# The depthwise convolution of the gated branch, issued step by step at a counted pace instead of with one late priority

## The chip, the core and the metric

The kernel runs on one NeuronCore of a Trainium2 chip. Five engines matter here: TensorE (matmuls, "PE" in the profile, its weight loads "PEld"), VectorE ("DVE"), ScalarE ("ACT"), GpSimd ("POOL") and SyncE ("SP", which only issues DMAs). Each works through its own instruction list in order and waits on semaphores for the others. The metric is the device time of one execution in microseconds. The kernel before the change takes 1662.74 us (median of 3 runs, 1662.30 to 1662.97).

## The reference, cut to what matters

```python
xn = rmsnorm(x, norm1_g)
proj = xn @ w_in
q, k, v, glu_a, glu_b, gate_a, gate_b = jnp.split(proj, SPLIT_IDX, axis=-1)
# branch A: sliding-window attention -> @ w_o_attn
u = glu_a * jax.nn.sigmoid(glu_b)                    # branch B, 1024 channels
u_ext = jnp.concatenate([conv_b_past, u], axis=1)    # 30 earlier rows
c = dwconv_valid(u_ext, conv_b_w, conv_b_bias)       # causal depthwise convolution, 31 taps
branch_b = jax.nn.silu(layernorm(c, ln_b_g, ln_b_b)) @ w_pb
merged = jax.nn.sigmoid(gate_a) * branch_a + jax.nn.sigmoid(gate_b) * branch_b
h = x + merged @ w_out
# then a feed-forward block with a 3-tap convolution, and a final RMSNorm
```

There are 1024 prompt tokens and 8 samples of 8 tokens, so 1088 columns, all in float32. A matmul is done as three: operands are split into a high part and a remainder, and high x high, high x remainder and remainder x high are added in PSUM (`mm3`, L201 to L203).

## The kernel before

**Stages.** The first stage (up to 649 us of the profile) is the input projection: 44 weight units of 128x1024 are streamed one after the other. The first five units, whose streams are interleaved, are not touched by the change. Every later unit but the two of the values makes one *stream*: three column chunks of 384, 384 and 320, eight contraction steps each, so 24 steps of three matmuls. The order of the units is the table `SEQUENCE`; `b` and `a` are the two halves of a gated unit (eight pairs, 0 to 7), `g` a gate, `q0`, `q1`, `k0`, `k1`, `v` the attention operands of two groups of heads. The later stages (attention output, branch-B projection, output projection, feed-forward) are not touched.

**What VectorE does in the first stage.** It takes the remainder of each weight unit (L183, `wlo`, after ScalarE has made the high part `whi`, L182), empties PSUM for q, k, v and the gated half (L731, L753, L231 `v`, L686), does most of the softmax (L330, L337), the remainders of the attention operands (L231 `ptl`, L388 `av`), and the convolution. One convolution (function `conv`, one of eight) has two products and two sums for the sample rows (L489, L490), one sum of neighbours (L491), 44 multiply-adds over 512 or 513 elements (L483; tiles `bt` and `c`) and four closing instructions (L502 to L505), 53 vector instructions in all. It ends with two stores to DRAM (`d_c`). Its three starting products are made on ScalarE.

**Buffers.** Two weight pairs (`whi`/`wlo` 0 and 1) alternate: the split of the next unit can begin once the unit before the present one has been streamed, and has to be done when its own stream starts. Two `u` tiles alternate between the eight gated units, so a convolution must be finished and stored before the unit two places on writes its `u`. PSUM has four `mm` banks, one for each chunk, and four `aux` banks for the attention.

**What sets the order.** The program is recorded in Python; each instruction gets a priority from its place in the record, and a scheduler at build time then arranges every engine's list, preferring what was recorded early among what it believes to be ready. `later(n)` lowers the priority of a block by n places. Small attention steps are planned on an agenda and recorded by `tick()`, which `stream` calls at each contraction step; `do_v`, which streams the two value units in nine blocks, doesn't call it. The whole of a convolution is recorded when its gated unit is complete (`a_done`, L689 to L694), under `later(CONV_LATER)` with 1200 places, so the scheduler fills it in wherever VectorE has nothing of better priority.

Of the kernel before, what the change touches and what calls it, by code (L numbers as in the profile page):

```python
# [74 lines left out]
CONV_LATER = 1200  # L75
# [45 lines left out]
class Build:  # L121
    def __init__(self, tc, a):
        self.tc, self.nc, self.a = tc, tc.nc, a
        self.order, self.n_in = weight_order()
        self.uid = 0
        self.agenda, self.now = [], 0

# [333 lines left out]
    def tick(self, upto=None):  # L461
        self.now = self.now + 1 if upto is None else upto
        while self.agenda and self.agenda[0][0] <= self.now:
            self.agenda.pop(0)[1]()

# [5 lines left out]
    def conv(self, i, u):  # L471
        nc = self.nc
# [13 lines left out]
        for x in range(2):  # L486
            win = us[:, 4 * x:4 * x + 4, 0:NT]
            win = bass.AP(tensor=win.tensor, offset=win.offset, ap=[list(z) for z in win.ap] + [[1, CW]])
            nc.vector.tensor_tensor(prod, win, taps, ALU.mult)  # L489
            nc.vector.tensor_reduce(sp[:, 4 * x:4 * x + 4, :], prod, AX.X, ALU.add)  # L490
        nc.vector.tensor_tensor(sm, od[:, 0:half + 15], ev[:, 1:half + 16], ALU.add)  # L491
# [4 lines left out]
        for j in range(1, 16):  # L496
            mac(bt, ev[:, j:j + half + 1], h(2 * j))
            if j < 15:
                mac(ye, od[:, j:j + half], h(2 * j + 1))
            mac(yo, sm[:, j:j + half], hs(j))  # L500
        out = u[:, NS:NS + SEQ]
        nc.vector.tensor_scalar(u[:, 0:NS], acc[:, SEQ:], self.c("cb", i), None, ALU.add)  # L502
        nc.vector.tensor_tensor(yo, yo, bt[:, 1:], ALU.subtract)
        nc.vector.tensor_tensor(out[:, 1::2], yo, ye, ALU.subtract)
        nc.vector.tensor_tensor(out[:, 0::2], ye, bt[:, 0:half], ALU.add)  # L505
# [136 lines left out]
    def phase_x(self):  # L642
# [17 lines left out]
        def u_start(i):  # L660
            u = self.t(self.cv, [P, UW], "u", bufs=2)
            nc.gpsimd.memset(u[:, 0:HIST], 0.0)
            nc.gpsimd.memset(u[:, HIST + SEQ:PW], 0.0)
            nc.sync.dma_start(u_views(u)[:, :, 0:HIST], a["cbT"][i])
            return u
# [23 lines left out]
        def a_done(i, u):  # L689
# [3 lines left out]
            with self.later(CONV_LATER):  # L693
                self.conv(i, u)  # L694
# [125 lines left out]
        u = u_start(0)  # L820
# [18 lines left out]
        for c in range(3):  # L839
# [9 lines left out]
            keep = [lambda c, o, n, ps, ev=ev: held.append(lambda: ev(c, o, n, ps)) for ev in evs]  # L849
# [68 lines left out]
    def phase_y(self, right, a0_es, states, ah, al):  # L918
# [22 lines left out]

        steps = []
# [864 lines left out]
```

## Time and profile before

| what | us |
|---|---|
| median of the runs | 1662.74 |
| the profiled execution, its own time | 1661.67 |
| its span, first to last instruction | 1659.9 |
| ACT busy in the span | 892.3 (54%) |
| POOL busy in the span | 318.4 (19%) |
| DVE busy in the span | 1338.7 (81%) |

The page gives busy time by engine, then the span in 40 slices with a digit for the busy tenths of each, then the chain of work that ended last, then groups of equal instructions. The trace can be asked for waits (who waited for whom, in total), for windows (busy time of each engine in a stretch) and for the timeline (instructions in order with the idle time ahead of them). The timeline's lines have start and duration in us, engine, source line, operation, output and inputs. [...]

### The profile page before, as it was taken

How to read it: one execution, taken by the hardware profiler on the slowest of the kernel's cores; microseconds unless marked ns; L12 is line 12 of the kernel's file. 1: busy time of each engine (PE TensorE's matmuls, PEld its weight loads, DVE VectorE, ACT ScalarE, POOL GpSimd, SP SyncE). 2: the span in 40 equal slices, each digit the busy share in tenths (PEclk: the TensorE clock that was granted, in tenths of full speed). 3: DMA queues.
4: the chain of work that ended last, by engine and by line, in shares of the span. 5: the costliest groups of instructions: out<-in, count | busy, mean ns of one | idle time of the engine just before them, and what ended most of it. 6: DMA issues, size and time to landing. Idle time of an engine off the chain costs nothing.

```text
span 1659.9 us, 30349 instructions
## 1 busy us (share of the span) xinstructions
PE 1641.4 (99%) x11616; PEld 1623.9 (98%) x11616; DVE 1338.7 (81%) x2432; ACT 892.3 (54%) x1819; POOL 318.4 (19%) x589
## 2 busy tenths in 40 slices
PE   9999999999999999999999999999999999999998
PEld 9999899999999999999999999999999999999998
DVE  8999988999769995875676897877777778968546
ACT  7524377753388754993353564444444446834322
POOL 0400222151211211110000123333433221000050
PEclk9999999999999999999999999999999999999999
DMA  6122135163421255545346527676777544856473
GB/s 213 46 48 71 60 94 136 48 200 82 124 67 49 66 192 189 176 137 187 120 126 204 134 71 212 182 182 176 182 176 176 144 112 142 288 158 220 137 147 119
DMA packets 121746, 232.12 MB, mean 140 GB/s; under 512 B 25457, under 2 KB 68097, under 8 KB 121169
## 3 DMA queue, kind: packets, MB, share of 16 engines
q1 hardware_dynamic: 88496, 140.01, 27.4%
q0 software_dynamic: 32384, 89.51, 21.3%
q8 instruction: 91, 1.49, 0.4%
q10 hardware_dynamic: 720, 0.66, 0.1%
q14 instruction: 55, 0.44, 0.1%
HBM read 169.74 MB, written 89.62 MB: 156 GB/s over the span
## 4 chain that ended last, share of the span: by engine, by line
PE 83%; DVE 11%; ACT 3%; DMA 1%; issue 1%; SPq 0%; DVEq 0%; ACTq 0%
PE mm L201 20%; PE mm L202 20%; PE mm L203 20%; PE aux L201 6%; PE aux L203 6%; PE aux L202 6%; DVE c L483 3%; DVE bt L483 1%; PE aux L369 1%; DMA xr<-xT 1%; DVE q L731 1%; PE aux L359 1%; DVE wlo L183 1%; PE aux L381 1%; DVE xr L307 1%
## 5 line engine op out<-in xcount | busy, mean ns | idle before, releaser
L201 PE MATMUL mm<-xh,whi 128*128 128x384 f32 (+1 forms) x920 | 306.7, 333 | 2.9 <-ACT kd L754 1.6
L203 PE MATMUL mm<-xh,wlo 128*128 128x384 f32 (+1 forms) x920 | 300.6, 327 | 0.0
L202 PE MATMUL mm<-xl,whi 128*128 128x384 f32 (+1 forms) x920 | 300.5, 327 | 0.0
L201 PEld LDWEIGHTS mm<-xh,whi 128*128 128x128 f32 x920 | 173.0, 188 | 5.1 <-ACT kd L754 1.9
L202 PEld LDWEIGHTS mm<-xl,whi 128*128 128x128 f32 x920 | 173.2, 188 | 0.8
L203 PEld LDWEIGHTS mm<-xh,wlo 128*128 128x128 f32 x920 | 172.7, 188 | 0.1
L1225 DVE SCALAR_TENSOR_TENSOR acc<-st,fc,acc 128x1104 f32<-128x1104 f32 x88 | 119.5, 1362 | 8.7 <-ACT acc L1223 7.9
L182 ACT CAST whi<-wraw 128x1024 fp32r<-128x1024 f32 (+1 forms) x65 | 62.6, 969 | 55.8 <-PE mm L202 49.6
L483 DVE SCALAR_TENSOR_TENSOR bt<-u,consts,bt 128x513 f32<-128x513 f32 x120 | 89.7, 748 | 0.6
L483 DVE SCALAR_TENSOR_TENSOR c<-sm,hsum,c 128x512 f32<-128x512 f32 x120 | 89.5, 746 | 0.5
L183 DVE TENSOR_TENSOR wlo<-wraw,whi 128x1024 fp32r<-128x1024 f32 (+1 forms) x65 | 73.3, 1134 | 20.1 <-ACT whi L182 19.7
L483 DVE SCALAR_TENSOR_TENSOR c<-u,consts,c 128x512 f32<-128x512 f32 x112 | 83.5, 746 | 0.3
L230 ACT CAST wlo<-th 128x512 fp32r<-128x512 f32 x56 | 35.1, 626 | 65.1 <-PE aux L203 41.4
L1394 ACT COPY st<-mm 128x272 f32<-128x272 f32 (+2 forms) x133 | 44.4, 350 | 46.7 <-PE mm L203 46.7
L201 PE MATMUL mm<-th,whi 128*128 128x272 f32 x240 | 69.3, 289 | 0.0
L203 PE MATMUL mm<-th,whi 128*128 128x272 f32 x240 | 69.3, 289 | 0.0
L202 PE MATMUL mm<-tl,whi 128*128 128x272 f32 x240 | 69.1, 288 | 0.0
L335 ACT ACTIVATE p<-p,nm 128x257 f32<-128x257 f32 (+1 forms) x128 | 62.2, 490 | 12.0 <-DVE nm L330 11.2
L1373 DVE TENSOR_TENSOR st<-st,aux 128x272 f32<-128x272 f32 (+2 forms) x95 | 34.2, 379 | 38.0 <-PE aux L203 38.0
L203 PE MATMUL mm<-sh,wlo 128*128 128x384 f32 (+1 forms) x192 | 62.6, 326 | 0.0
L202 PE MATMUL mm<-sl,whi 128*128 128x384 f32 (+1 forms) x192 | 62.6, 326 | 0.0
L201 PE MATMUL mm<-sh,whi 128*128 128x384 f32 (+1 forms) x192 | 62.6, 326 | 0.0
(651 smaller groups left out, 5896.1 us busy)
## 6 DMA issues: line engine op xcount, KB each, us to landing
wraw<-wall SPq DMA_DIRECT2D x87, 512.0 KB, 3.9
d_x<-st POOLq DMA_DIRECT2D x27, 544.0 KB, 5.3
d_wd<-wall POOLq DMA_DIRECT2D x54, 256.0 KB, 6.2
th<-wall SPq DMA_DIRECT2D x18, 512.0 KB, 6.2
wraw<-wall SPq DMA_DIRECT2D x33, 256.0 KB, 4.3
x<-d_x SPq DMA_DIRECT2D x14, 544.0 KB, 4.6
d_x<-acc POOLq DMA_DIRECT2D x9, 816.0 KB, 7.3
d_wo<-wall POOLq DMA_DIRECT2D x24, 256.0 KB, 4.8
```

Source lines behind the costliest of these rows:

```text
L182: self.nc.scalar.copy(h[:, z], r[:, z])
L183: self.nc.vector.tensor_tensor(l[:, z], r[:, z], h[:, z].bitcast(F32), ALU.subtract)
L201: mm(ps, wh, xh, start=first, stop=False, skip_group_check=more)
L202: mm(ps, wh, xl, start=False, stop=False, skip_group_check=more)
L203: mm(ps, wl, xh, start=False, stop=last, skip_group_check=more)
L230: self.nc.scalar.copy(h, src)
L307: nc.vector.scalar_tensor_tensor(x, x, self.c("g1", k), rstd[:, :CHUNKS[c][1]], ALU.mult, ALU.mult)
L335: nc.scalar.activation(pt[:, j, lo:width + 1], pt[:, j, lo:width + 1], AF.Exp, bias=nm[:, j:j + 1], scale=-1.0, accum_out=den[:, j:j + 1])
L483: mac = lambda o, x, w: nc.vector.scalar_tensor_tensor(o, x, w, o, ALU.mult, ALU.add)
L1225: self.last_tap = nc.vector.scalar_tensor_tensor(acc, st[:, k:k + AW], fw(f, k), acc, ALU.mult, ALU.add)
L1373: plus = lambda d, s: nc.vector.tensor_tensor(d, d, s, ALU.add)
L1394: op(d, r(ps))
```

## The change

The convolution becomes a generator: `yield` stands between its vector instructions, and `a_done` only appends it to a list `convs`. After every `tick()`, the new `pace()` looks at what was recorded since the last time, adds 0.172 to a number `room` for each TensorE instruction and takes 0.5 off for each VectorE one, caps it at 1.4, and records convolution steps, at 0.68 each, while it is above zero. Each step is tied behind the VectorE instruction recorded last (`issue_after`), and stands 30 places later in priority instead of 1200. `conv_flush(1)` at the start of a gated unit records all that is left of every convolution but the youngest, and `conv_flush()` ahead of the LayerNorm the rest.

```diff
-CONV_LATER = 1200
+PE_STEP, DVE_STEP, CONV_STEP = 0.172, 0.5, 0.68
+ROOM = 1.4
+PACE_LATER = 30
...
         while self.agenda and self.agenda[0][0] <= self.now:
             self.agenda.pop(0)[1]()
+        self.pace()
+
+    def pace(self):
+
+        traced, pe, dve = self.nc.cur_bb.bb.instructions, self.nc.tensor.engine, self.nc.vector.engine
+        for ins in list(traced)[self.seen:]:
+            if ins.engine == pe:
+                self.room += PE_STEP
+            elif ins.engine == dve:
+                self.room -= DVE_STEP
+        self.seen = len(traced)
+        self.room = min(self.room, ROOM) if self.convs else 0
+        while self.convs and self.room > 0:
+            self.conv_step()
+            self.room -= CONV_STEP
+        self.seen = len(traced)
+
+    def conv_step(self):
+        with ExitStack() as es:
+            dve = self.nc.vector.engine
+            es.enter_context(self.tc.issue_after(next(x for x in reversed(list(self.nc.cur_bb.bb.instructions)) if x.engine == dve)))
+            es.enter_context(self.later(PACE_LATER))
+            if next(self.convs[0], None) is None:
+                self.convs.pop(0)
+
+    def conv_flush(self, keep=0):
+        while len(self.convs) > keep:
+            self.conv_step()
...
             nc.vector.tensor_tensor(prod, win, taps, ALU.mult)
+            yield 1
             nc.vector.tensor_reduce(sp[:, 4 * x:4 * x + 4, :], prod, AX.X, ALU.add)
+            yield 1
...
         for j in range(1, 16):
+            yield 1
             mac(bt, ev[:, j:j + half + 1], h(2 * j))
+            yield 1
             if j < 15:
                 mac(ye, od[:, j:j + half], h(2 * j + 1))
+                yield 1
             mac(yo, sm[:, j:j + half], hs(j))
+        yield 1
...
         def u_start(i):
+            self.conv_flush(1)
...
-            with self.later(CONV_LATER):
-                self.conv(i, u)
+            self.convs.append(self.conv(i, u))
...
+        self.conv_flush()
         steps = []
         for x in range(KT):
             steps += self.ln_steps(x, self.now + LN_LEAD + x * LN_SPACING, sh, sl)
```

Both programs hold the same instructions (11454 on TensorE, 2434 on VectorE); only the order differs, and only in the first stage. Source lines of the changed kernel stand a little further down: L515 there is the multiply-add L483 of before, L186 the weight remainder L183, L234 the remainder L231, L204 to L206 the matmuls L201 to L203, L541 to L545 the closing instructions L503 to L505. Three places of the built order follow.

VectorE while the two value units are streamed; `v` is the emptying of one block of values, `c`, `bt` and `u` belong to convolutions. Before:

```order
L231 TENSOR_TENSOR v_951<-mm_1809,v_951 128x2x128
L483 SCALAR_TENSOR_TENSOR bt_1138<-u_954,consts_77,bt_1138 128x513
L483 SCALAR_TENSOR_TENSOR c_1136<-sm_1137,hsum_86,c_1136 128x512
L502 TENSOR_SCALAR u_954<-c_1136,consts_77 128x64
L503 TENSOR_TENSOR c_1136<-c_1136,bt_1138 128x512
L505 TENSOR_TENSOR u_954<-c_1136,bt_1138 128x512
L231 TENSOR_TENSOR v_951<-mm_1836,v_951 128x2x128
L504 TENSOR_TENSOR u_954<-c_1136 128x512
L491 TENSOR_TENSOR sm_1681<-u_1502 128x527
L489 TENSOR_TENSOR c_1680<-u_1502,consts_77 128x992
L231 TENSOR_TENSOR v_951<-mm_1863,v_951 128x2x128
```

and now, with the weight remainder that comes next and the first softmax instruction of the attention:

```order
L234 TENSOR_TENSOR v_890<-mm_1778,v_890 128x2x128
L234 TENSOR_TENSOR v_890<-mm_1805,v_890 128x2x128
L234 TENSOR_TENSOR v_890<-mm_1832,v_890 128x2x128
L234 TENSOR_TENSOR v_890<-mm_1859,v_890 128x2x128
L186 TENSOR_TENSOR wlo_185_1924<-wraw_1664,whi_184_1923 128x1024
L333 ISA p_1928,nm_1940<-aux_1929,masks_891,nsink_84 128x128
```

Before, 24 convolution instructions stand between the first and the last of the eight `v` rows; now none does.

VectorE at the change from stream `b` to stream `a` of gated unit 5, where `wlo_505` is the weight remainder of that `a` (the pair `whi_504`, `wlo_505`). Before:

```order
L231 TENSOR_TENSOR q_27_123<-aux_3974,q_26_122 64x4x16
L483 SCALAR_TENSOR_TENSOR c_3409<-sm_3410,hsum_86,c_3409 128x512
L231 TENSOR_TENSOR q_27_123<-aux_3974,q_26_122 64x4x16
L483 SCALAR_TENSOR_TENSOR bt_3411<-u_3052,consts_77,bt_3411 128x513
L483 SCALAR_TENSOR_TENSOR c_3409<-u_3052,consts_77,c_3409 128x512
L483 SCALAR_TENSOR_TENSOR c_3409<-sm_3410,hsum_86,c_3409 128x512
L483 SCALAR_TENSOR_TENSOR bt_3411<-u_3052,consts_77,bt_3411 128x513
L483 SCALAR_TENSOR_TENSOR c_3409<-u_3052,consts_77,c_3409 128x512
L183 TENSOR_TENSOR wlo_505_4026<-wraw_3889,whi_504_4025 128x1024
```

and now:

```order
L515 SCALAR_TENSOR_TENSOR bt_3761<-u_2991,consts_77,bt_3761 128x513
L515 SCALAR_TENSOR_TENSOR c_3759<-u_2991,consts_77,c_3759 128x512
L515 SCALAR_TENSOR_TENSOR c_3759<-sm_3760,hsum_86,c_3759 128x512
L234 TENSOR_TENSOR q_27_123<-aux_3936,q_26_122 64x4x16
L515 SCALAR_TENSOR_TENSOR bt_3761<-u_2991,consts_77,bt_3761 128x513
L515 SCALAR_TENSOR_TENSOR c_3759<-u_2991,consts_77,c_3759 128x512
L234 TENSOR_TENSOR q_27_123<-aux_3936,q_26_122 64x4x16
L515 SCALAR_TENSOR_TENSOR c_3759<-sm_3760,hsum_86,c_3759 128x512
L515 SCALAR_TENSOR_TENSOR bt_3761<-u_2991,consts_77,bt_3761 128x513
L515 SCALAR_TENSOR_TENSOR c_3759<-u_2991,consts_77,c_3759 128x512
L515 SCALAR_TENSOR_TENSOR c_3759<-sm_3760,hsum_86,c_3759 128x512
L186 TENSOR_TENSOR wlo_505_3993<-wraw_3839,whi_504_3992 128x1024
```

The rows look alike, but before, `wlo_505` was placed when TensorE was at the third of the 24 steps of stream `b`, one stream ahead of its use; now it stands where TensorE is already in stream `a`.

TensorE at the same place. Before, the stream of `a` starts in its plain form:

```order
L203 MATMUL mm_4081<-xh_24_108,wlo_491_3892 128x320
L201 MATMUL mm_4118<-xh_20_104,whi_504_4025 128x384
L202 MATMUL mm_4118<-xl_21_105,whi_504_4025 128x384
L203 MATMUL mm_4118<-xh_20_104,wlo_505_4026 128x384
L201 MATMUL mm_4118<-xh_20_104,whi_504_4025 128x384
```

and now:

```order
L206 MATMUL mm_4060<-xh_24_108,wlo_491_3842 128x320
L204 MATMUL mm_4103<-xh_20_104,whi_504_3992 128x384
L205 MATMUL mm_4103<-xl_21_105,whi_504_3992 128x384
L204 MATMUL mm_4134<-xh_22_106,whi_504_3992 128x384
L205 MATMUL mm_4134<-xl_23_107,whi_504_3992 128x384
L204 MATMUL mm_4166<-xh_24_108,whi_504_3992 128x320
L205 MATMUL mm_4166<-xl_25_109,whi_504_3992 128x320
L204 MATMUL mm_4210<-xh_20_104,whi_510_4099 128x384
L205 MATMUL mm_4210<-xl_21_105,whi_510_4099 128x384
L206 MATMUL mm_4103<-xh_20_104,wlo_505_3993 128x384
```

Ahead of the first matmul that needs `wlo_505`, the first two matmuls of all three chunks, and of the stream after (`whi_510`), have been pulled forward into the four `mm` banks.

More of the change, by code (lines that the diff above doesn't have):

```diff
@@ L126, in __init__ @@
         self.agenda, self.now = [], 0
+        self.convs, self.seen, self.room = [], 0, 0
     @contextmanager
@@ L503, in conv @@
         nc.vector.tensor_tensor(yo, yo, bt[:, 1:], ALU.subtract)
+        yield 1
         nc.vector.tensor_tensor(out[:, 1::2], yo, ye, ALU.subtract)
+        yield 1
         nc.vector.tensor_tensor(out[:, 0::2], ye, bt[:, 0:half], ALU.add)
```

## The prediction

> **What bounds the kernel now.** I read the head of the page first.
>
> ```profile
> span 1659.9 us, 30349 instructions
> PE 1641.4 (99%) x11616; PEld 1623.9 (98%) x11616; DVE 1338.7 (81%) x2432; ACT 892.3 (54%) x1819; POOL 318.4 (19%) x589
> DVE  8999988999769995875676897877777778968546
> PEclk9999999999999999999999999999999999999999
> ```
>
> TensorE is busy 99% of the span at full clock. The change takes no matmul away, so it can gain at most what TensorE idles, and only where convolutions stand. VectorE is near full in the first ten slices, up to 415 us. So next came windows over the first stage, cut at the end of the first five streams (72.9 us), at the value units, and at the end of the streams before `k1` (443.5 us).
>
> ```profile
> 72.90:120.30 47.40, 47.40 (x290) 47.40 (x289) 46.92 (x68) 13.82 (x28) 10.91 (x13) 1.00 0.18 38
> 120.30:185.30 65.00, 62.12 (x435) 61.23 (x434) 63.61 (x97) 24.38 (x51) 5.00 (x12) 1.00 0.23 72
> 185.30:258.60 73.30, 68.82 (x438) 65.45 (x437) 64.84 (x156) 54.55 (x145) 18.10 (x30) 1.00 0.32 87
> 258.60:360.50 101.90, 101.90 (x659) 98.78 (x658) 98.22 (x212) 74.07 (x182) 31.22 (x62) 1.00 0.44 125
> 360.50:443.50 83.00, 83.00 (x506) 83.00 (x506) 80.69 (x121) 26.33 (x49) 18.43 (x33) 1.00 0.41 102
> 443.50:649.00 205.50, 205.17 (x1313) 200.39 (x1313) 164.37 (x367) 144.15 (x357) 33.44 (x65) 1.00 0.38 118
> ```
>
> After length come the busy us of PE, PEld, DVE, ACT and POOL, each with its count. From 72.9 to 443.5 us VectorE is busy 354.3 of 370.6 us (the sum of its column in five rows): this stretch has two engines at their limit, TensorE and VectorE, and VectorE has 16.3 us to spare. The waits of TensorE in the first stage show what that costs.
>
> ```profile
> PE aux L359 <- DVE ptl L231: 3.5, 2, 3.0
> PE mm L201 <- ACT kd L754: 1.6, 1, 1.6
> PE mm L201 <- ACT qs L736: 1.3, 1, 1.3
> PE aux L381 <- DVE ptl L231: 0.6, 1, 0.6
> PE aux L382 <- DVE ptl L231: 0.3, 1, 0.3
> ```
>
> Total, times, longest: 7.3 us in six waits. Two are on ScalarE's copies of q and k, which alternate with VectorE's (L731, L753); the rest are on VectorE directly. The longest one, in VectorE's timeline:
>
> ```profile
> 197.47 0.75 DVE L483 SCALAR_TENSOR_TENSOR c<-sm,hsum,c 128x512 f32<-128x512 f32 x1
> ...
> 205.50 0.69 DVE L231 TENSOR_TENSOR ptl<-aux,pth 128x512 fp32r<-128x512 f32 x1
> ```
>
> and from ScalarE's and TensorE's:
>
> ```profile
> 201.88 0.57 ACT L230 CAST pth<-aux 128x512 fp32r<-128x512 f32 x1
> 206.24 0.39 PE L359 MATMUL aux<-kd,q 128*128 128x256 f32 x1 [3.00 <-DVE ptl L231]
> ```
>
> ScalarE's half was done at 202.45, but `ptl` started at 205.50: from 197.47 on VectorE worked through twelve multiply-adds of a convolution. VectorE was late, and the convolution stood ahead of the attention.
>
> **What one instruction costs.** The distances from start to start:
>
> ```profile
> 429.73 0.75 DVE L483 SCALAR_TENSOR_TENSOR bt<-u,consts,bt 128x513 f32<-128x513 f32 x1
> ...
> 436.36 0.75 DVE L483 SCALAR_TENSOR_TENSOR c<-sm,hsum,c 128x512 f32<-128x512 f32 x1
> 437.03 1.22 DVE L183 TENSOR_TENSOR wlo<-wraw,whi 128x1024 fp32r<-128x1024 f32 x1
> 438.17 0.25 DVE L502 TENSOR_SCALAR u<-c,consts 128x64 f32<-128x64 f32 x1
> ```
>
> Eleven multiply-adds from 429.73 to 437.03 make 0.664 us each, about 0.085 under the duration; a weight remainder takes 1.14. A remainder of q, which alternates with ScalarE, leaves no overlap (0.59 to the next start, 0.04 over its duration):
>
> ```profile
> 109.45 0.55 DVE L731 TENSOR_TENSOR q<-mm,q 64x384 fp32r<-64x384 f32 x1
> 110.04 0.76 DVE L483 SCALAR_TENSOR_TENSOR c<-u,consts,c 128x512 f32<-128x512 f32 x1
> ```
>
> For the rest I take 0.085 off the mean of the groups (the number behind the busy time):
>
> ```profile
> L731 DVE TENSOR_TENSOR q<-mm,q 64x384 fp32r<-64x384 f32 (+1 forms) x22 | 11.4, 519 | 1.7 <-ACT q L730 1.1
> L489 DVE TENSOR_TENSOR c<-u,consts 128x992 f32<-128x992 f32 x2 | 2.4, 1188 | 0.0
> L686 DVE TENSOR_TENSOR u<-mm,u 128x384 f32<-128x384 f32 (+2 forms) x4 | 1.7, 435 | 0.0
> L503 DVE TENSOR_TENSOR c<-c,bt 128x512 f32<-128x512 f32 x2 | 1.4, 686 | 0.0
> L491 DVE TENSOR_TENSOR sm<-u 128x527 f32<-128x527 f32 x6 | 4.2, 699 | 0.0
> L388 DVE TENSOR_TENSOR av<-aux,av 64x512 f32<-64x512 f32 x16 | 11.0, 687 | 1.9 <-ACT av L387 1.7
> ```
>
> TensorE's pace, from a window row of line L203 alone and from its timeline:
>
> ```profile
> 372.30:443.50 71.20, 47.01 (x145) 27.03 (x144) 1.00 0.39 94
> 379.88 0.33 PE L203 MATMUL mm<-xh,wlo 128*128 128x384 f32 x1
> 380.05 0.33 PE L201 MATMUL mm<-xh,whi 128*128 128x384 f32 x1
> 381.09 0.31 PE L201 MATMUL mm<-xh,whi 128*128 128x320 f32 x1
> 381.23 0.30 PE L202 MATMUL mm<-xl,whi 128*128 128x320 f32 x1
> ```
>
> The window row counts L203 alone: 144 weight loads, so six streams (a stream has 24 steps with one L203 each), in 71.2 us or 11.87 each. By the last four rows a matmul takes 0.17 us at 384 columns and 0.14 to 0.15 at 320.
>
> [...]
>
> **What goes.** TensorE's waits between 130 and 250 us come from VectorE being behind. The new order puts nothing of the convolutions into the value units, where before 24 of them stand. There VectorE is full now:
>
> ```profile
> 159.60:185.30 25.70, 25.70 (x219) 25.70 (x218) 25.67 (x43) 3.88 (x8) 2.66 (x6) 1.00 0.18 61
> ```
>
> Without 24 x 0.66 = 16 us of these 25.67 it catches up any lag and enters the attention on time. The 13 convolution instructions between the first softmax and the first `ptl` stay (the built order has them, twelve before), but start earlier by that lag, which was over the 3.05 us from 202.45 to 205.50. I take 6.3 of the 7.3 us as gone and 1.0 as left; the bounds are 7.3, and 2.9 if only the two waits at q and k go.
>
> **What comes.** `pace` is called by `tick`, and the value streams don't tick; `room` is capped, so those 16 us are not made up at once. The same 53 instructions per convolution must still be done before unit i+2, and VectorE's spare time was 16.3 us. By the built order the debt falls due late. Until the `b` stream of unit 5, VectorE's rows and TensorE's sum to nearly the same. From there on, two steps.
>
> First, `wlo_505`. From the last attention combine there (`av`) to the end of the split, VectorE has: `av` 0.60, one L490 1.10, L491 0.61, the remainder of q 0.60 and two small ones 0.3, twelve multiply-adds 7.97, the split 1.14: 12.3 us. TensorE, from the same place to the matmul that needs it: 21 matmuls at 0.173, 25 at 0.147 and seven small ones under 0.11: 7.8 us, the pulled-forward ones included. TensorE waits **4.5 us**. Behind that matmul is all of TensorE's list; it can't go on with anything else. With VectorE ahead by 1 us it is 3.5, with the lag seen before (3 us) 7.5.
>
> Second, from the end of `wlo_505` to the end of `wlo_550` (needed by the sixth stream after), the order has 115 vector instructions: 76 multiply-adds 50.5, six splits 6.8, four L489/L490 4.4, seven closing or opening ones 3.6, four L686 1.4, 18 L731 (twelve of 384 columns at 0.59, six of 256 with 0.42 + 0.04) 9.8: 76.5 us. TensorE has 5.875 streams, 69.7 us. Before, each split stood a stream ahead, and VectorE's small lag cost nothing; now each stands within 0 to 2 us of its use, so the difference becomes TensorE's waits: **6.8 us**. Bounds: 4.2 if the copies of q overlap as other instructions do and VectorE is 1 us ahead at the start, 8.5 with the idle time of 1.7 us that the L731 row has for 22 of them.
>
> Third, during the attention, `wlo_385` now stands immediately ahead of the matmul that needs it: one split, **1.1 us** (0 to 3). Its neighbour `wlo_412` has 1.7 us, enough for itself.
>
> After 443.5 us VectorE has 41 us to spare and the splits stand further ahead (2 us in one place, over 4 elsewhere); by the built order the LayerNorm's first load moves by 4 us, with some 6 before its matmul. I count these at nothing; without that cover, 1 to 2 us.
>
> **The sum.** -6.3 + 4.5 + 6.8 + 1.1 = +6.1 us. The profiled execution took 1661.67 us (span 1659.9); it becomes 1667.8. The median of the runs lies 1.07 above it: 1662.74 + 6.1 = **1668.8**. As a second way, VectorE's own account up to 443.5 us: 16.3 us idle before; now about 12 in the value units, 2 ahead of the first convolution (there is little else for it then), some 6 to 9 of waits in the attention: 20 to 23, that is +4 to +7.
>
> **Rivals.**
> - *The catch-up is hidden.* The waits that I remove go and the late splits cost nearly nothing, because VectorE runs ahead of the built order (convolution steps wait for no matmul). For: before, windows 258 to 443 us show TensorE without idle time at 96% VectorE. Against: each split stands behind 11 to 18 convolution instructions in its own queue, which is in order. It decides once VectorE is 4.5 us ahead of the built order at `wlo_505` and 11.3 at `wlo_550`. Time: 1662.7 - 6.3 = 1656.4.
> - *Even.* Only the wait at `wlo_505` and the one in the attention come, and the second step is absorbed by VectorE's being early at its start: -6.3 + 4.5 + 1.1, so 1662.0; with half of the second step 1665.4.
> - *Stores and banks.* Unit 4's `u` now waits for the last step of convolution 2, which stands at the end of its `b` stream, and for its store. From issue to landing:
>
> ```profile
> DMA to landing us min/median/max: 1.7/3.9/8.5
> ```
>
>   Three banks hold that `b` stream, one is left for `a`, and a chunk of 384 is 4.1 us. Beyond that the store shows as idle TensorE: 0 at the median, 4.4 at the maximum. With it and 1.5 us after 443.5: 1674.7.
> - *It does not do what it says.* Pacing counts in recorded instructions; a flush instead of pacing would give bursts. The built order has singles spaced by three or four matmuls in most streams, and the exception is where I price it.
>
> **Numbers.** My forecast (1666 to 1671) 0.57; stores and banks 0.16; even 0.19; hidden 0.08. About 0.2% (3.3 us, the limits are 1659.4 and 1666.1) is what a measurement of this kernel can tell from no change. Slower takes the first two, 0.73; the same 0.19; faster 0.08. The range for 8 in 10 goes from 1662.5 (-7.3, 3.5, 4.2 and nothing in the attention make +0.4, and the even case lies at its lower end) to 1675.5 (just over the stores).
>
> **What will show it.** Right: the waits at q, k and `ptl` before 250 us gone; VectorE at 40 to 60% in the value units; one TensorE wait of 4 to 5 us on `wlo` at the sixth gated unit, then waits of about 1 us on `wlo` at each of the next five streams; VectorE without a gap there. Wrong: TensorE's waits on `wlo` under 3 us in total, which would mean that VectorE got ahead, or a long wait at the start of the attention, which would mean that lag was not its cause.

## The result, and the profile after

The changed kernel takes **1682.05 us** (median of 4 runs, 1680.50 to 1683.72), the kernel before 1662.52 us beside it (4 runs): a ratio of 1.0118, 95% interval 1.0100 to 1.0136. The profiled execution took 1681.15 us, 19.48 more than the one profiled before. The direction was forecast; the size, 6.1 us, was a third of it, and the time lies above the range.

The head of the page, as it was shown of before:

```profile
span 1679.4 us, 30315 instructions
PE 1649.6 (98%) x11616; PEld 1628.6 (97%) x11616; DVE 1337.3 (80%) x2432; ACT 894.5 (53%) x1819; POOL 323.2 (19%) x589
DVE  8989699999959995775666787887777778977556
PEclk9999999999999999999999999999999999999999
```

VectorE does the same work (1337.3 us against 1338.7). TensorE is busy 8.2 us longer with the same matmuls, though the clock row shows nothing: its slices are 42 us long. The windows below are cut at the same stream steps as before (the first column is the time at which the same matmul starts).

```profile
72.90:120.00 47.10, 47.10 (x288) 47.10 (x287) 40.39 (x59) 16.24 (x34) 9.84 (x13) 1.00 0.22 52
120.00:185.20 65.20, 62.36 (x438) 61.98 (x437) 53.18 (x82) 23.99 (x49) 5.36 (x11) 1.00 0.25 64
185.20:251.50 66.30, 66.18 (x431) 64.49 (x430) 63.13 (x144) 48.88 (x127) 16.86 (x28) 1.00 0.34 90
251.50:352.00 100.50, 99.07 (x632) 94.45 (x632) 95.23 (x212) 73.13 (x184) 28.63 (x50) 1.00 0.43 108
352.00:454.00 102.00, 93.65 (x540) 91.40 (x539) 98.68 (x151) 31.25 (x61) 26.76 (x49) 0.95 0.42 112
454.00:660.40 206.40, 206.11 (x1315) 200.41 (x1314) 165.59 (x371) 144.94 (x357) 34.15 (x63) 1.00 0.34 105
```

In the first two stretches VectorE (third pair) is busy 93.6 us where it was busy 110.5: 17 us of its work aren't done there any more. The fifth stretch is 102.0 us long where it was 83.0, with 34 more matmuls, 30 more vector instructions and a mean granted clock of 0.95. TensorE's waits from 100 to 760 us:

```profile
PE aux L564 <- DVE red L557: 4.9, 1, 4.9
PE mm L206 <- DVE wlo L186: 4.3, 2, 3.0
PE mm L204 <- ACT qs L776: 2.6, 1, 2.6
PE mm L204 <- DVE v L234: 2.3, 1, 2.3
PE aux L435 <- ACT sp L342: 1.1, 1, 1.1
PE mm L204 <- ACT u L717: 0.8, 1, 0.8
PE mm L204 <- DVE q L771: 0.6, 1, 0.6
PE mm L204 <- DVE u L727: 0.6, 1, 0.6
```

None of the waits of before is left, and 17.2 us of others have come. They lie in three places: the value units (`u` L727 and `v`, 2.8 us), the stretch from the attention to 454 us (`wlo`, `sp`, `u` L717, `qs`, `q`, 9.4 us), and the first mean of the LayerNorm (`red`, 4.9 us). The clock is halved three times behind such waits (each time is one record of the trace, called a half-clock record below):

```profile
374.89:381.72 6.83, 5.79 (x18) 5.80 (x19) 6.83 (x10) 0.00 (x0) 1.64 (x4) 0.50 0.34 103
415.85:419.26 3.41, 3.25 (x10) 3.25 (x11) 3.38 (x6) 0.11 (x1) 0.83 (x1) 0.50 0.55 192
671.85:675.26 3.41, 3.37 (x11) 3.40 (x12) 2.21 (x4) 1.66 (x2) 0.00 (x0) 0.50 0.00 0
```

What that does to a matmul is seen in TensorE's timeline behind the wait for `wlo`:

```profile
375.93 0.69 PE L206 MATMUL mm<-xh,wlo 128*128 128x384 f32 x1 [3.05 <-DVE wlo L186]
...
378.01 0.52 PE L206 MATMUL mm<-xh,wlo 128*128 128x384 f32 x1
378.33 0.52 PE L204 MATMUL mm<-xh,whi 128*128 128x384 f32 x1
...
382.86 0.34 PE L205 MATMUL mm<-xl,whi 128*128 128x384 f32 x1
383.03 0.34 PE L206 MATMUL mm<-xh,wlo 128*128 128x384 f32 x1
```

From start to start it is 0.32 us at half clock and 0.17 at full. The three records hold 18, 10 and 11 matmuls, which cost 0.147 us more each: 2.7, 1.5 and 1.6 us.

### The profile page after: what moved, and what is told of

Same layout as the page of the kernel before. It is cut to its first block, busy times and chain, and to the rows that moved or that the text cites. A ratio compares the mean times of both kernels' runs of the same rounds, so it can differ in the third digit from the quotient of the medians.

```text
span 1679.4 us, 30315 instructions
## 1 busy us (share of the span) xinstructions
PE 1649.6 (98%) x11616; PEld 1628.6 (97%) x11616; DVE 1337.3 (80%) x2432; ACT 894.5 (53%) x1819; POOL 323.2 (19%) x589
## 5 line engine op out<-in xcount | busy, mean ns | idle before, releaser
L204 PE MATMUL mm<-xh,whi 128*128 128x384 f32 (+1 forms) x920 | 306.3, 333 | 4.0 <-ACT qs L776 2.6
L206 PE MATMUL mm<-xh,wlo 128*128 128x384 f32 (+1 forms) x920 | 304.3, 331 | 4.5 <-DVE wlo L186 4.3
L205 PE MATMUL mm<-xl,whi 128*128 128x384 f32 (+1 forms) x920 | 304.0, 330 | 0.0
L204 PEld LDWEIGHTS mm<-xh,whi 128*128 128x128 f32 x920 | 174.5, 190 | 6.3 <-ACT qs L776 3.2
L206 PEld LDWEIGHTS mm<-xh,wlo 128*128 128x128 f32 x920 | 174.3, 190 | 6.0 <-DVE wlo L186 5.4
L515 DVE SCALAR_TENSOR_TENSOR bt<-u,consts,bt 128x513 f32<-128x513 f32 x120 | 89.9, 749 | 0.4
L515 DVE SCALAR_TENSOR_TENSOR c<-sm,hsum,c 128x512 f32<-128x512 f32 x120 | 89.7, 747 | 0.3
L515 DVE SCALAR_TENSOR_TENSOR c<-u,consts,c 128x512 f32<-128x512 f32 x112 | 83.6, 747 | 1.2 <-ACT c L528 0.9
L186 DVE TENSOR_TENSOR wlo<-wraw,whi 128x1024 fp32r<-128x1024 f32 (+1 forms) x65 | 73.4, 1135 | 13.8 <-ACT whi L185 12.5
L206 PE MATMUL mm<-th,whi 128*128 128x272 f32 x240 | 69.5, 290 | 0.0
L204 PE MATMUL mm<-th,whi 128*128 128x272 f32 x240 | 69.5, 289 | 0.0
L206 PE MATMUL mm<-sh,wlo 128*128 128x384 f32 (+1 forms) x192 | 62.7, 327 | 0.0
L204 PE MATMUL mm<-sh,whi 128*128 128x384 f32 (+1 forms) x192 | 62.7, 326 | 0.0
```

Of the source, the lines that this page charges most:

```text
L186: self.nc.vector.tensor_tensor(l[:, z], r[:, z], h[:, z].bitcast(F32), ALU.subtract)
L204: mm(ps, wh, xh, start=first, stop=False, skip_group_check=more)
L205: mm(ps, wh, xl, start=False, stop=False, skip_group_check=more)
L206: mm(ps, wl, xh, start=False, stop=last, skip_group_check=more)
L515: mac = lambda o, x, w: nc.vector.scalar_tensor_tensor(o, x, w, o, ALU.mult, ALU.add)
```

## The experiments

TensorE executes the same 3552 stream steps in the same order in all of these kernels, so a kernel's lead or lag can be read at every step (its start against the same step of the kernel before). These steps are numbered 1 to 3552 below; "the stretch" is from step 553 to step 769, which is 321.7 to 454.4 us in the changed kernel. All times beside an experiment are medians, and the kernel before ran beside each at 1662.4 to 1663.0 us. In the first four expectations, P is the theory that the price comes of the place of the steps (30 places behind, so ahead of weight splits and copies), D the theory that it comes of the debt which the value units leave, because no step is given out there.

**The splits sooner.** The remainder of each weight unit was given a better priority, so that none stands close to its use in the built order.

```diff
-            self.nc.vector.tensor_tensor(l[:, z], r[:, z], h[:, z].bitcast(F32), ALU.subtract)
+            with self.later(-SPLIT_SOONER):   # 600
+                self.nc.vector.tensor_tensor(l[:, z], r[:, z], h[:, z].bitcast(F32), ALU.subtract)
```

> The changed kernel with one edit: VectorE's part of each weight split is recorded 600 places sooner in priority, so the scheduler puts it ahead of waiting convolution steps (in the built order each split stands 7 to 18 us ahead of its use again). The convolution keeps its 30 places. Theory P (the convolution steps' priority puts splits and attention behind them, and that is the price): TensorE's waits on wlo and the two half-clock stretches between 370 and 420 us go, the delay gained from the first attention to the end of the q streams falls from +11 us to about +2, and the run takes 1670 to 1674 us; the 4.9 us wait ahead of the LayerNorm stays, because the attention still ends late. Theory D (the convolution work left out in the value streams is a debt of VectorE that must be paid whatever the order): the waits move to other instructions (emptying of q, banks) and the time stays at 1679 to 1683 us.

Measured 1680.23 us (1678.17 to 1682.02), ratio 1.0106 (1.0093 to 1.0120): nearly nothing gained. No wait on a split `wlo` of this stage is left, but VectorE's and TensorE's timelines show what took its place (L517 is the multiply-add here, L729 the emptying of a bank of the gated half):

```profile
384.87 0.74 DVE L517 SCALAR_TENSOR_TENSOR c<-sm,hsum,c 128x512 f32<-128x512 f32 x1
...
396.14 0.75 DVE L517 SCALAR_TENSOR_TENSOR c<-u,consts,c 128x512 f32<-128x512 f32 x1
396.91 0.56 DVE L729 TENSOR_TENSOR u<-mm,u 128x384 f32<-128x384 f32 x1
```

```profile
397.53 0.69 PE L206 MATMUL mm<-xh,whi 128*128 128x384 f32 x1 [10.59 <-DVE u L729]
```

Eighteen multiply-adds stand in a row ahead of the copy that frees a bank, and TensorE waits 10.59 us for the bank instead of 3.05 for the remainder, with 13.65 us of half clock around it. So the wait on `wlo` was a symptom: VectorE was that far behind, and whichever of its customers stands last pays.

**Steps in the value units too.**

```diff
                 for k in range(KT):
+                    self.pace()
                     wh, wl = ws[k // 4]
```

> The changed kernel with the pacing also called at each step of the value blocks, so that about 20 more convolution steps are recorded there. Theory D: with the debt gone the catch-up costs nothing, the delay from the first attention to the end of the q streams falls from +11 us to 0 or below, the run takes 1668 to 1672 us. Theory P: the splits during and after the attention still stand behind convolution steps (0 to 3 us ahead of their use at four of the streams), so one or two waits on wlo stay; 1673 to 1678 us. In both the wait ahead of the LayerNorm stays at 4 to 6 us.

Measured 1683.33 us (1680.07 to 1684.30): both theories missed. The debt was indeed gone (at step 361, 88 multiply-adds were done, against 90 before and 70 in the changed kernel), yet from step 409 to 505 TensorE went from 11.5 us ahead of the kernel before to 4.4 us behind it. A part of this is only moved work: 45 of the attention's matmuls, which the kernel before does ahead of step 409, stand between the two steps here. The rest is lost. There multiply-adds stand between the remainders `ptl` of the attention:

```profile
232.75 0.69 DVE L234 TENSOR_TENSOR ptl<-aux,pth 128x512 fp32r<-128x512 f32 x1
233.36 0.74 DVE L515 SCALAR_TENSOR_TENSOR c<-u,consts,c 128x512 f32<-128x512 f32 x1
234.02 0.75 DVE L515 SCALAR_TENSOR_TENSOR c<-sm,hsum,c 128x512 f32<-128x512 f32 x1
234.68 0.68 DVE L234 TENSOR_TENSOR ptl<-aux,pth 128x512 fp32r<-128x512 f32 x1
```

and three waits of 0.8, 1.0 and 3.1 us (the last on ScalarE's `sp`) come with 10.24 us of half clock. So the loss doesn't need the debt.

**All steps late.** `PACE_LATER` is 1200 as before the change; generator, ties and pacing stay.

```diff
-PACE_LATER = 30
+PACE_LATER = 1200
```

> The changed kernel with 1200 places instead of 30 for each convolution step, the single steps and their tie to the record unchanged. Theory P: splits stand a stream ahead of their use again, the attention of the second group ends where it did before the change, so the waits on wlo, the half-clock stretches and the wait ahead of the LayerNorm all go, and what is gained at q and k before the value streams (3 us) stays: 1657 to 1664 us. Theory D: the value streams still hold no convolution, so the debt stays, and only the part ahead of the LayerNorm goes: 1672 to 1677 us.

Measured **1660.05 us** (11 runs, 1658.36 to 1661.85), ratio 0.9986 (0.9977 to 0.9995). The whole loss hangs on that number. The debt is still there (70 multiply-adds at step 361, as in the changed kernel). What became of it shows in windows over the stretch and over the attention behind it, first of before, then of the changed kernel, then of this one:

```profile
329.80:443.90 114.10, 114.10 (x702) 113.40 (x701) 110.76 (x181) 46.20 (x99) 34.03 (x62) 1.00 0.49 131
443.90:527.10 83.20, 82.94 (x534) 80.31 (x533) 57.31 (x145) 68.60 (x176) 12.95 (x26) 1.00 0.28 74
```

```profile
321.70:454.40 132.70, 124.35 (x734) 120.82 (x733) 127.70 (x221) 55.85 (x127) 33.55 (x60) 0.96 0.44 113
454.40:537.40 83.00, 82.83 (x533) 80.27 (x532) 59.54 (x151) 68.71 (x176) 13.00 (x26) 1.00 0.28 74
```

```profile
320.70:434.80 114.10, 114.10 (x702) 113.41 (x702) 110.41 (x179) 45.66 (x98) 30.95 (x56) 1.00 0.46 126
434.80:523.90 89.10, 86.22 (x535) 82.14 (x534) 75.70 (x174) 68.98 (x177) 13.77 (x27) 0.98 0.24 64
```

The stretch takes TensorE 114.1 us, and VectorE was already busy for 110.8 of them. The changed kernel puts 127.7 us of vector work into it, 40 instructions more, and it becomes 18.6 us longer. Only 20 of the 40 are multiply-adds; nearly all the others belong to the first attention (17 softmax instructions, 4 `ptl`), which the convolution steps had held back: at step 553, 22 `ptl` are done, where the kernel before has 26. Of the 18.6 us, 8.4 are waits and 4.2 half clock; the rest, some 6 us, is the time of 32 matmuls of that attention which are done earlier in the kernel before, and is not lost. With 1200 places the attention is not held back (26 `ptl` at step 553), and the surplus of multiply-adds slides out behind the stretch, where VectorE had 26 us to spare: there the multiply-adds of the convolution rise from 15 to 38 (the rows of that line alone, before and with all late), and it costs 5.9 us.

```profile
443.90:527.10 83.20, 10.52 (x15) 1.00 0.28 74
```

```profile
434.80:523.90 89.10, 26.34 (x38) 0.98 0.24 64
```

**All late, with steps in the value units.** The two edits together.

> Both: 1200 places, and the pacing called in the value blocks too. Theory P: VectorE is used in the value streams and nothing stands behind convolution steps, 1655 to 1662 us, at or a little below the kernel before. Theory D: the debt is gone, but nothing else, so about the same as the run with the value blocks alone, less the wait ahead of the LayerNorm: 1662 to 1667 us.

Measured 1659.58 us (11 runs, 1658.10 to 1663.73), ratio 0.9984 (0.9975 to 0.9993), the lowest of all. With hardly any debt left (85 multiply-adds at step 361) it is not told apart from the run before. Set beside the run with steps in the value units at 30 places, it shows what the place does without the debt. From step 553 to 769 the two have 95 and 96 multiply-adds, but at 30 places the attention comes late again (22 `ptl` at step 553, against 26): VectorE has 120.7 us of work there instead of 111.5, and TensorE takes 126.3 us instead of 114.1, with 5.2 us of waiting and a half-clock record of 6.8 us among them.

**The first six units against the last two.** A counter `ended` of finished convolutions chooses the priority.

```diff
-            es.enter_context(self.later(PACE_LATER))
+            es.enter_context(self.later(PACE_LATER if self.ended < 6 else 1200))   # last two late
+            es.enter_context(self.later(PACE_LATER if self.ended >= 6 else 1200))  # or: first six late
```

> The changed kernel, but the convolution steps of the last two of the eight units (the ones that run beside the second attention, up to the LayerNorm) are put back to 1200 places behind, and the first six keep 30. Theory O (each stretch pays for its own order): TensorE is some 10.5 us behind the kernel before at its 769th stream step, as in the changed kernel, then loses nothing more; the 4.9 us wait for red at the LayerNorm and the half-clock record behind it are gone, and the time is 1670 to 1675 us. Theory L (the wait at the LayerNorm is lateness carried over from the first attention): the wait of 4 to 5 us stays, 1679 to 1683 us.

> The reverse: the first six units' convolution steps 1200 places behind, the last two 30. Theory O: TensorE is about 3 us ahead of the kernel before at its 889th stream step, as with all eight late, then pays 5 to 7 us at the LayerNorm and 1 to 2 us at the stage behind it: 1665 to 1671 us. Theory L: with no lateness carried over there is no wait at the LayerNorm above 1 us: 1658 to 1662 us. By theory O the losses of this run and of the one with the last two late add up to that of the changed kernel against the one with all late, 22 us.

Measured 1675.14 us (1673.49 to 1676.72), ratio 1.0080 (1.0064 to 1.0097), with the last two late; 1666.61 us (8 runs, 1665.84 to 1668.16), ratio 1.0025 (1.0015 to 1.0036), with the first six late. With the last two late TensorE stands 11.3 us behind at step 769, 11.5 at step 1105, and waits for nothing between 560 and 760 us. With the first six late it is 2.6 us ahead at step 1090 and then:

```profile
PE aux L565 <- DVE red L558: 3.7, 1, 3.7
```

with a half-clock record behind it, 6.3 us in all. So the wait at the LayerNorm is not lateness carried over; the steps of the last two units make it themselves. The losses against the kernel with all late, 15.1 and 6.6 us, add up to 21.7; the changed kernel loses 22.0.

**The sigmoid ahead of the LayerNorm.** In the changed kernel ScalarE and VectorE show this at that place:

```profile
664.40 1.11 ACT L973 ACTIVATE ga<-ga 128x1088 f32<-128x1088 f32 x1 [7.09 <-DMA ga<-d_ga]
665.42 1.03 ACT L185 CAST whi<-wraw 128x1024 fp32r<-128x1024 f32 x1
```

```profile
666.49 1.22 DVE L186 TENSOR_TENSOR wlo<-wraw,whi 128x1024 fp32r<-128x1024 f32 x1 [2.08 <-ACT whi L185]
667.74 1.29 DVE L575 TENSOR_TENSOR ct<-ct,aux 128x1088 f32<-128x1088 f32 x1
```

ScalarE stands 7.09 us at the sigmoid of a gate tile until its load lands; the cast `whi`, VectorE's `wlo`, the centering and `red` follow. Two edits tried to take the sigmoid out of the way; the first placed it 60 places later, the second tied it behind the ScalarE instruction recorded last:

```diff
+                if m == 1:
+                    es.enter_context(tc.issue_after(next(x for x in reversed(list(nc.cur_bb.bb.instructions)) if x.engine == nc.scalar.engine)))
                 nc.scalar.activation(t, t, AF.Sigmoid)
```

> The changed kernel, with the sigmoid of the second gate tile ga placed 60 places later on ScalarE, so that the cast and the square of the first LayerNorm block stand ahead of it. Theory S (ScalarE stands at that sigmoid until the load of ga lands at 664.4 us, and VectorE's centering and red wait behind the cast): the wait of 4.9 us at the first mean of the LayerNorm falls below 1.5 us, the half-clock record at 671.85 us is gone, 1673 to 1677 us. Theory C (the load of the LayerNorm block itself, landed at 653.6 us, and VectorE's queue set it): the wait stays above 3 us, 1679 to 1683 us.

> The changed kernel, with the sigmoid of the second gate tile tied behind the last ScalarE instruction that is written ahead of it, so that in the program's order it now stands behind the cast and the square of the first LayerNorm block (the run e5_ga_later left the order as it was). Theory S (ScalarE stands at that sigmoid until the load of ga lands, VectorE's centering and red wait behind the cast): red no longer waits for 664.4 us, the wait of 4.9 us falls below 1.5 us with no half-clock record behind it, and the time is 1673 to 1677 us. Theory C (the load of the LayerNorm block and VectorE's queue set it): the wait stays above 3 us, 1679 to 1683 us.

The first left the order as it was, so its 1680.72 us (1679.50 to 1681.24) say nothing of either theory. The second took 1681.24 us (1677.83 to 1683.89), which can't be told from the changed kernel; its trace shows the place, though. The cast now starts at 659.80, and what is left ahead of the remainder is VectorE's wait for the load of the second LayerNorm block (4.01 us in the changed kernel, ended at 663.21):

```profile
663.35 0.72 DVE L557 TENSOR_TENSOR part<-u 128x544 f32<-128x544 f32 x1 [3.94 <-DMA u<-d_c]
664.11 0.44 DVE L557 TENSOR_TENSOR part<-part 128x272 f32<-128x272 f32 x1
664.46 1.22 DVE L186 TENSOR_TENSOR wlo<-wraw,whi 128x1024 fp32r<-128x1024 f32 x1
```

```profile
669.86 0.47 PE L564 MATMUL aux<-red,mean 128*128 128x136 f32 x2 [3.26 <-DVE red L557]
```

TensorE still waits 3.26 us, without a half-clock record behind it; the loss from step 1081 to 1105 falls from 6.56 to 3.30 us. So both theories hold a part: the sigmoid set the end, but with it out of the way the load of the second LayerNorm block sets one only 1.7 us sooner. That load is late for the reason that the gate's is. SyncE's own waits in the changed kernel between 600 and 670 us have

```profile
SPq L569 <- DMA d_c<-u: 7.3, 1, 7.3
```

Its queue, in order, stands at the first LayerNorm load until the last convolution is stored, issues it at 653.64 us, and the second block's load and the gate's come behind (655.51 and 655.93). With all steps late the first two of these stand at 633.21 and 633.68, and the gate loads ahead of them, at 612.67 and 613.12, though SyncE stands for the last store there too (8.1 us).

**Matmuls that only keep TensorE busy.** 16, then 22 matmuls of the `mean` tile with itself ahead of the first mean of the LayerNorm.

```diff
+            for _ in range(warm):   # 16, or 22, at the first block
+                nc.tensor.matmul(ps[:, 0:P], self.mean, self.mean, start=True, stop=True)
             nc.tensor.matmul(ps[:, :n], self.mean, live["red"], start=True, stop=True)
```

> The changed kernel with 16 matmuls of the mean tile with itself, whose product is overwritten, put ahead of the first mean of the LayerNorm, so that TensorE works while it stands there (some 0.27 us each, 4.3 of the 4.9 us). Theory K (the clock is halved because TensorE stood still in most of a stretch of 3.41 us): red arrives at the same time, the record of half clock at 671.85 us is gone, and 1.5 to 2 us are saved in the trace between the 1090th and the 1105th stream step; 1679 to 1681 us. Theory W (the halving has another cause, such as load): the record stays, and the time is 1681 to 1684 us.

> As e10_warm, with 22 instead of 16 of the extra matmuls (0.22 us each there, 4.9 us), since 16 left TensorE idle for 2.57 us of one stretch of 3.41 us, and the half clock came. Theory K (the clock is halved after a stretch of 3.41 us in which TensorE stood for more than 1.5 to 2 us): less than 1.5 us of idle time stays, there is no half-clock record between 655 and 690 us, and the loss from the 1090th to the 1105th stream step is 4.5 to 5.5 us in place of the 6.56 us of the changed kernel; 1679 to 1681.5 us. Theory W (the record has another cause): it stays, and the loss is 6.5 us or more.

Measured 1682.82 us (1681.80 to 1685.58) and 1682.89 us (1680.69 to 1683.44): neither is told from the changed kernel. The traces, by a window over the place, first with 16 and then with 22:

```profile
655.00:690.00 35.00, 32.43 (x200) 32.14 (x199) 18.32 (x28) 18.18 (x24) 3.78 (x7) 0.95 0.63 190
```

```profile
655.00:690.00 35.00, 34.67 (x226) 34.38 (x226) 18.75 (x28) 18.55 (x25) 3.78 (x7) 1.00 0.64 204
```

With 16, 2.6 us of the wait stayed and the record too; the loss from step 1081 to 1105 was 7.8 us, so this run can't tell the theories apart. With 22 the wait is 0.3 us, the clock stays at 1.00, and the loss is 5.3 us in place of 6.56: theory K. Here the record of half clock came with 2.57 us of idle time on TensorE and not with 0.33. The gain of 1.2 us does not show in the median; that profile had two other records, at 64 and 173 us, which the changed kernel's did not have.

**Room counted by columns**, with the last two units late.

```diff
-                self.room += PE_STEP
+                self.room += max(0.11, 0.172 * cols / 384)
...
-                self.room -= DVE_STEP
+                self.room -= 0.06 + cols / 960
```

> As e8_last_two_late, but the room is counted by columns: a matmul gives 0.172 us per 384 columns (at least 0.11) in place of 0.172 for all, and a VectorE instruction takes 0.06 us and 1 us per 960 columns in place of 0.5 us for all, so that convolution steps are given out sooner where VectorE's instructions are short and less densely where they are long. The priority of 30 stays. Theory R (the loss of 20 us against the late steps, from the 409th to the 769th stream step, comes of how many steps the count gives out and when: too few early, too many beside the weight splits): the loss from the 505th to the 649th step, 15 us in e8_last_two_late, falls below 5 us, and the time is 1660 to 1669 us. Theory O (any step placed with priority 30 ahead of other vector work in the stretches where VectorE is full costs this much): 1672 to 1678 us.

Measured 1671.92 us (1670.90 to 1673.62), ratio 1.0056 (1.0040 to 1.0073), 3.2 us under the run with the last two late; the loss from step 505 to 649 is 13.3 us instead of 15.1. Theory R fell, and the time lies just under the range of theory O: sharing the steps out by a better count saves a little, and the stretch stays over-full.

```profile
321.00:448.90 127.90, 121.07 (x734) 117.89 (x734) 121.70 (x206) 55.41 (x125) 31.86 (x58) 0.99 0.42 113
```

VectorE has 121.7 us of work in 127.9. And one wait is new. ScalarE stands 3.35 us before it empties the first bank of a gated unit, until the store of the convolution that last used that `u` tile has landed; TensorE waits 4.6 us for the bank behind it:

```profile
377.37 1.26 ACT L721 COPY u<-mm 128x384 f32<-128x384 f32 x4 [3.35 <-DMA d_c<-u]
```

**Only the first three units at 30.**

```diff
+            es.enter_context(self.later(PACE_LATER if self.ended < 3 else 1200))
```

> The changed kernel with priority 30 for the convolution steps of the first three of the eight units only (done by the 503rd stream step); the steps of the last five stand 1200 places behind. Up to the 505th step it runs as the changed kernel does. Theory V (the loss of the first six units lies in one stretch, from the 553rd to the 769th stream step, where VectorE is full and the steps that came in late may not slide out behind it): that stretch takes 114 to 116 us in place of 132.7, with at most 97 multiply-adds in it in place of 109, TensorE stands 1 to 7 us ahead of the kernel before at the 889th step, and the time is 1657 to 1663 us. Theory O in its strict form (priority 30 costs wherever it stands, so the three units keep a part): the waits of the value stage (3.3 us) and of the first attention show in the end, 1664 to 1672 us.

Measured 1666.59 us (11 runs, 1664.86 to 1668.98), ratio 1.0023 (1.0014 to 1.0033). The main sign of theory V is there, 1 us above what it gave:

```profile
323.60:440.70 117.10, 117.10 (x723) 115.85 (x722) 112.46 (x182) 50.55 (x108) 31.78 (x58) 1.00 0.45 124
```

117.1 us instead of 132.7, with 92 multiply-adds instead of 110, and TensorE full in it. But at step 889 TensorE stands 3.0 us behind the kernel before, where theory V had it 1 to 7 us ahead, and the time is that of the strict theory O: the waits of the value units, with a half-clock record of 3.41 us that they drew in this run, are kept to the end (TensorE is 4.6 us behind the kernel with all late at step 361, and 6.7 at step 1105).

By difference of medians, the three parts of priority 30 against all late: the first three units 6.5 us, the fourth to sixth 8.6, the last two 6.9.

## Why the prediction was wrong, point by point

Half of the mechanism was seen: VectorE gets no convolution in the value units, falls into debt and makes it up beside the weight splits before 454 us, and TensorE waits there. But the debt, which the prediction gives as the reason, doesn't decide: with the debt and 1200 places the kernel takes 1660.05 us, without the debt and at 30 places 1683.33. What decides is the place of the steps, ahead of the attention and the splits, from where they can't slide out behind the full stretch. That the forecast of +12.4 us for this stretch came near the measured +14.0 is in part luck, as the points below show. In the sum, the step that failed most is "After 443.5 us VectorE has 41 us to spare ... I count these at nothing". TensorE's idle time in the two traces, by stretches, sets the terms against each other:

| term | predicted | measured |
|---|---|---|
| waits before 250 us | -6.3 | -4.4 (7.37 to 2.95 us of idle time) |
| waits from 250 to 460 us | +12.4 | +14.0 (9.77 us of idle time, 4.2 of half clock) |
| LayerNorm | 0 | +6.6 (4.9 and 1.6) |
| sum | +6.1 | +16.2 |

Of the 19.5 us, 1.6 come slowly between 866 and 950 us, where the two programs are alike, and the rest (1.7) is spread over small differences. In the other traces the same steps take from 0.4 us less to 1.0 us more than in the kernel before, so the 1.6 change from run to run; no run says what they are.

- **"I take 6.3 of the 7.3 us as gone"**: all 7.3 went. But "it catches up any lag and enters the attention on time" overlooked the entry into the value units. Steps recorded ahead of them stand in VectorE's queue before the copies that free TensorE's banks; the wait behind these multiply-adds is 2.28 us:

```profile
169.48 0.75 DVE L515 SCALAR_TENSOR_TENSOR bt<-u,consts,bt 128x513 f32<-128x513 f32 x1
170.14 0.75 DVE L515 SCALAR_TENSOR_TENSOR c<-u,consts,c 128x512 f32<-128x512 f32 x1
```

  The forecast of 40 to 60% for VectorE there was about right (18.08 of 29.4 us, 61%).
- **`wlo_505`, 4.5 us; `wlo_385`, 1.1 us**: 3.05 and 1.29 us were measured, at the places named. At the first, another 0.76 us of wait for ScalarE's `u` stands just ahead.
- **The catch-up, 6.8 us, as waits of about 1 us on `wlo` in the next five streams**: the size was near, the form wrong. Behind `wlo_505` one wait of 2.56 us came on `qs` and one of 0.6 on `q`, and half clock made the rest; 1.1 us more, on `sp`, came ahead of `wlo_505`, where the sum has nothing. The splits-sooner run shows that it doesn't matter which tile is named. That VectorE has no gap in the catch-up was right (78.5 us busy in the 79.65 from 374.65 to 454.3).
- **The LayerNorm, counted at nothing**: the prediction looked at the first load, at 4 us of delay against 6 us of cover. That load is issued 17.9 us later than before (653.64 against 635.79) while TensorE is 11.2 us later at step 1081, so its delay was 6.6 us. The load that set the end was another: the gate's load, which the new order puts in SyncE's queue behind the LayerNorm's, and through it ScalarE's sigmoid, on which VectorE hangs. VectorE's spare time was no cover, since VectorE was not working there but waiting (7.05 us for the first block's load, 4.01 for the second's). This is 6.6 of the 13.4 us missing; the waits before 250 us make 1.9, those behind 1.6, and the 3.3 us outside the table the rest.
- **Full clock throughout**: the sum priced a wait at its length. The three records of half clock add 5.8 us, which the measured terms of the table contain.
- **"stores and banks", 1674.7**: the place of this rival is real, as the run with room by columns shows (4.6 us), but it is not what decided here: in the changed kernel no copy into `u` on TensorE's path waits for a store, and the store counted at the LayerNorm instead.

The second way of the prediction, VectorE's account up to 443.5 us, gave +4 to +7 and failed likewise: it expected 20 to 23 us of idle time on VectorE, and by the first five window rows of the changed kernel there were 30.5 (381.1 us less 350.6 busy). Of these, 6.7 lie between 72.9 and 120.0 us, where it had put 2.

## What to carry to other kernels

Where two engines are both full over a stretch, work given to one of them has to be free to slide out of it, and must not stand ahead of what the other waits for: the same steps cost 22 us more at 30 places than at 1200. When one engine's filler is moved, follow the in-order queues of the others to the next stage (here a store for which SyncE's load queue stood 7.3 us, and a sigmoid at which ScalarE stood 7.09 us), and price a wait of the matmul engine at its length plus, where some 2 us of it can fall into one stretch of 3.41 us (in these traces all 27 with 1.97 us or more of idle time were followed by half clock), the matmuls that run at half clock behind it (1.5 to 2.7 us here). A wait's named tile is the customer who stood last: if the same engine is late for all, mending that tile moves the wait (3.05 us on `wlo` became 10.59 us on `u` with the splits sooner).

## What the hardware showed that was not expected

In the traces of this study TensorE's granted clock changed on a fixed grid of 3.41 us. In the changed kernel the records start at 374.89, 415.85 and 671.85 us, 12 and 75 times 3.413 us apart, whenever the waits began; in the 3.41 us ahead of each, TensorE was idle for 2.77, 2.39 and 3.41 us. Over the 14 traces of this study, with the grid read from each one's records, I counted TensorE's idle time in every such stretch that was entered at full clock (about 6,700, without the last 10 us of the span). All 27 with 1.97 us or more of idle time were followed by half clock; none with 1.40 us or less was; of those between, five were and 17 were not. So idle time of less than two thirds of a stretch was enough here (1.97 of 3.41 us). What a wait cost therefore hung on how it fell into the grid: the kernel before had one of 3.00 us at 206.24, which fell into two stretches as 1.53 and 1.54 us, and kept its clock; the kernel with the first three units at 30 had one of 2.27 us at 171.1, 2.11 of it in one stretch, and lost 3.41 us of full clock, where the changed kernel with the same wait (2.28 us, 1.09 and 1.19 of it in two stretches) did not. The runs of the kernels with long waits also scatter more (1677.8 to 1683.9 us for the tied sigmoid, against 1662.0 to 1663.4 for the kernel before beside it); that the clock is the reason is shown in part only. In the kernel with the first three units at 30, the five runs with a mean granted clock of 0.995 took 1667.12 to 1668.98 us and the six with 0.997 to 0.999 took 1664.86 to 1666.59; the four runs of the tied sigmoid have no such order.
